# Transposes of normalised tokens in a two-layer encoder: handed back by the normalisation and placed among the dense products

## The chip, the cores and the metric

The kernel runs on one core of one Trainium2 chip. TensorE (PE in the profile) multiplies matrices and transposes; VectorE (DVE), ScalarE (ACT) and GpSimd (POOL) do elementwise work; SyncE (SP) issues most transfers. Each engine executes its own list of instructions in order and waits on semaphores for the others. The metric is the device time of one execution in microseconds (us).

## The reference

The reference normalises the input and runs two layers. A layer feeds the normalised tokens to three branches (pooling, differential attention with a relative-position bias, and a bidirectional RWKV-7 time mix), gates and merges them, projects, adds the residual and normalises; then a squared-ReLU MLP, residual and normalisation again:

```python
x = layer_norm(x, ln0_g, ln0_b)
for l in range(DEPTH):
    mix = hybrid_mixer(x, w_in[l], ...)
    x = layer_norm(alpha * x + mix, ln1_g[l], ln1_b[l])
    hid = jnp.square(jax.nn.relu(jnp.einsum('bsd,df->bsf', x, w_up[l])))
    x = layer_norm(alpha * x + jnp.einsum('bsf,fd->bsd', hid, w_down[l]), ln2_g[l], ln2_b[l])
```

There are 512 tokens, width 1024, an MLP of width 4096; all in float32.

## The kernel before

Every wide product is computed three times over with split operands: `split` (lines 142 and 143) makes a high part on ScalarE and the remainder on VectorE or GpSimd, and `mm3` (lines 181 to 183) issues high times high, high times low and low times high. The dense products need the tokens with the channels on the partitions: `self.xh` and `self.xl`, eight tiles of 128 channels by 512 tokens.

Three stages make these tokens anew: the end of `project` in layers 0 and 1, and the end of `mlp` in layer 0. All work alike. `token_tiles` runs the last products of four token tiles (128 tokens each; 24 products of 512 columns a tile) and calls `finish` after each, which calls `ln_tile`. That adds the residual with the row sums (line 238, VectorE), takes squares (L243, ScalarE), forms the scale (L245, L247, GpSimd), and writes the normalised row in two halves of 512 channels. For tiles 0 to 2 the first half is done by VectorE (L249, L256) and the second by GpSimd in three products (L252 to L254); tile 3 is done by VectorE alone. For each half four transposes follow on TensorE (L262, into one bank of PSUM), a cast to `xh` on ScalarE (L267) and a subtraction to `xl` on VectorE (L268). The banks of the four tiles are d l, a t, d l, a c, so that "d<-cst,s" in a row is the first half of tile 0 or 2.

Behind `token_tiles` stands `dense_halves`: three dense products (banks d, l, a), first for tokens 0 to 255, which need tiles 0 and 1, then for tokens 256 to 511. That is 2 x 3 x 24 = 144 products of 256 columns. In `mlp` these are the low-rank inputs of the next layer; `rw_prep` takes them over with `shift`, applies tanh and splits them with `lora_inputs` (L571 to L573), and goes on to the dense products for keys, inputs and values.

The order on each engine is not that of the code. The program is handed to a scheduler that simulates its own timeline and lays down every engine's list; the code's order is one of its inputs. Pools with a fixed number of buffers (`acc` takes the banks in turn) add waits for the last reader of a buffer.

Of the kernel before, what the change touches and what calls it, by code (L numbers as in the profile page):

```python
# [13 lines left out]
AF = mybir.ActivationFunctionType  # L14
ALU = mybir.AluOpType
# [7 lines left out]
NT = S // 128  # L23
DFF = 4096
# [6 lines left out]
LN_EPS = 1e-5  # L31
# [16 lines left out]
ALL_BANKS = "dlatdlac"  # L48
# [73 lines left out]
class Enc:  # L122
# [73 lines left out]

    def dense_halves(self, wts, tags="dl"):

        wts = [next(wts) for _ in tags]
        pss = [self.acc(t) for t in tags]  # L200
        for h in range(2):
            t = slice(h * 256, h * 256 + 256)
            for ps, (wh, wl) in zip(pss, wts):
                for k in range(NK):
                    if isinstance(wh, list):
                        h, l = wh[k // 4][:, k % 4, :], wl[k // 4][:, k % 4, :]
                    else:
                        h, l = wh[:, k, :], wl[:, k, :]
                    self.mm3(ps[:, t], h, l, self.xh[:, k, t], self.xl[:, k, t], k == 0, k == NK - 1)
        return pss  # L210
# [15 lines left out]

    def ln_tile(self, L, s, add, gb, it, eps, dst, transpose=True, banks="tc", bufs=2, pool=False):

# [21 lines left out]
        for h in range(2):  # L250
# [6 lines left out]
            if dst is not None:  # L257
                nc.sync.dma_start(dst[it * 128:(it + 1) * 128, half[h]], s[:, half[h]])
            if transpose:
                ps = self.acc(banks[h])  # L260
                for k in range(4):
                    nc.tensor.transpose(ps[:, k * 128:(k + 1) * 128], s[:, (h * 4 + k) * 128:(h * 4 + k + 1) * 128],  # L262
                                        self.ident)
                pv = ps.rearrange("p (k t) -> p k t", k=4)
                xh = self.xh[:, h * 4:h * 4 + 4, it * 128:(it + 1) * 128]
                xl = self.xl[:, h * 4:h * 4 + 4, it * 128:(it + 1) * 128]
                A.copy(xh, pv)  # L267
                V.tensor_tensor(xl, pv, xh, ALU.subtract)  # L268


    def run(self):
        tc, nc, a = self.tc, self.nc, self.a
        V, A, G = nc.vector, nc.scalar, nc.gpsimd
        with ExitStack() as ctx:
# [14 lines left out]
            with tc.tile_pool(name="LW", bufs=1, side="right") as LW, tc.tile_pool(name="L0", bufs=1, side="right") as L:  # L289
# [13 lines left out]
                for it in range(2):  # L303
                    self.ln_tile(L, ss[it], None, gb, it, LN_EPS, self.xs, banks=("tc", "ll")[it], bufs=NT, pool=it == 1)
                wts = [self.split(raws[i], [128, NK, 128], LW, "w", 3, G) for i in range(3)]
                for it in range(2, NT):
                    self.ln_tile(L, ss[it], None, gb, it, LN_EPS, self.xs, banks=("aa", "tc")[it - 2], bufs=NT)
                self.early = [self.wload(a["w_in"][0][:, COL_Z + i * 128:COL_Z + (i + 1) * 128], NK, 128) for i in (4, 0)]
# [156 lines left out]
    def rw_prep(self):  # L465
# [5 lines left out]
        pss = self.lora_ps  # L471
# [11 lines left out]
        yield 10.4  # L483
        tl = self.shift(pss[0], 12, self.F, "mg", 8)
        A.activation(tl, tl, AF.Tanh)
        tl = self.lora_inputs("tl", tl)
        la = self.lora_inputs("la", self.shift(pss[1], 13, self.F, "mg", 8))
        zg = self.shift(pss[2], 14, self.F, "mg", 8)
        A.activation(zg, zg, AF.Tanh, scale=0.5)
        V.tensor_scalar(self.sg, zg, 0.5, 0.5, ALU.mult, ALU.add)  # L490
        yield 5.2
        kw, rw, vw = (self.zcols(4 * i, 4) for i in (1, 0, 2))
        for j in range(4):
# [5 lines left out]
            yield 5.6  # L499
            if j == 0:  # L500
                ws = self.T(self.F, [128, 4, S], "ybh", 1, F32R)
                w2 = self.lora_weights([ws[:, i] for i in (0, 1)], a["rw_w2"][l])
                a2 = self.lora_weights([ws[:, i] for i in (2, 3)], a["rw_a2"][l])
# [719 lines left out]

    def token_tiles(self, X, xs, src, r0, finish, ahead):


        wr = []
        for k2 in range(0, 4, 2):
            for n in range(2):
                raw = self.wload(src[r0 + k2 * 128:r0 + (k2 + 2) * 128, n * 512:(n + 1) * 512], 2, 512)  # L1230
                wr.append(self.split(raw, [128, 2, 512], X, "wr", 4, self.nc.gpsimd))
        ahead()
        for it in range(NT):
            t = slice(it * 128, it * 128 + 128)
            for n in range(2):
                for k in range(4):
                    wh, wl = wr[k // 2 * 2 + n]
                    self.mm3(self.accs[it][n], xs[k][0][:, t], xs[k][1][:, t], wh[:, k % 2, :], wl[:, k % 2, :], False, k == 3)
            finish(it)

    def project(self):
# [21 lines left out]
        def finish(it):  # L1263
            self.ln_tile(L, self.s[it], self.accs[it], gb, it, 4.0 * LN_EPS, None, True,
                         ALL_BANKS[2 * it:2 * it + 2], pool=it < 3)

        with tc.tile_pool(name=f"W{l}", bufs=1) as X:
# [3 lines left out]

            self.token_tiles(X, self.mgr[4:], a["w_out"][l], 512, finish, ahead)
            self.up_ps = self.dense_halves(iter(self.ahead), "dla")

    def mlp(self):
# [4 lines left out]
        with tc.tile_pool(name=f"H{l}", bufs=1) as H, tc.tile_pool(name=f"M{l}", bufs=1) as M:  # L1280
            gb = self.ln_params(L, a["ln2_g"][l], a["ln2_b"][l])
            for half in range(2):
# [43 lines left out]
                def finish(it):  # L1326
                    self.ln_tile(L, self.s[it], self.accs[it], gb, it, LN_EPS, self.out[0] if last else self.xs, not last,
                                 ALL_BANKS[2 * it:2 * it + 2], pool=it < 3)

# [4 lines left out]

                self.token_tiles(M, hid[-4:], a["w_down"][l], DFF - 512, finish, ahead)
                if not last:
                    self.lora_ps = self.dense_halves(iter(self.ahead), "dla")

# [30 lines left out]
```

## Time and profile before

| | |
|---|---|
| median of three timed runs | 2115.34 us (2114.27 to 2118.49) |
| profiled execution | 2121.15 us |
| its span | 2119.4 us |
| TensorE busy | 2024.2 us, 96% of the span |
| TensorE's mean granted clock | 0.971 of full speed |

The span is the profiled time from first to last instruction. A row of a timeline gives the start, the duration and the instruction; in brackets stands how long the engine had been idle and who released it. Durations of matmuls overlap, so the distance between two starts is what one costs.

### The profile page before, as it was taken

How to read it: one execution, taken by the hardware profiler on the slowest of the kernel's cores; microseconds unless marked ns; L12 is line 12 of the kernel's file. 1: busy time of each engine (PE TensorE's matmuls, PEld its weight loads, DVE VectorE, ACT ScalarE, POOL GpSimd, SP SyncE). 2: the span in 40 equal slices, each digit the busy share in tenths (PEclk: the TensorE clock that was granted, in tenths of full speed). 3: DMA queues.
4: the chain of work that ended last, by engine and by line, in shares of the span. 5: the costliest groups of instructions: out<-in, count | busy, mean ns of one | idle time of the engine just before them, and what ended most of it. 6: DMA issues, size and time to landing. Idle time of an engine off the chain costs nothing.

```text
span 2119.4 us, 32782 instructions
## 1 busy us (share of the span) xinstructions
PE 2024.2 (96%) x13502; PEld 1647.4 (78%) x13502; DVE 1017.7 (48%) x1672; ACT 855.4 (40%) x1345; POOL 642.3 (30%) x447
## 2 busy tenths in 40 slices
PE   7999999899999999999989998989999999999998
PEld 5777778677787888888777676877777878888886
DVE  5775854445404542343348739454356045423433
ACT  5544554554233332232335336454532333312322
POOL 4555412122545200000536543021225561000004
PEclk9999989999999999999999999789999999999999
DMA  6446213455444233332424562135553442333322
GB/s 210 154 149 215 86 50 92 125 159 151 120 166 122 59 92 100 92 97 96 148 80 153 156 193 76 31 97 154 145 152 114 153 119 67 93 100 91 98 96 84
DMA packets 319042, 250.70 MB, mean 118 GB/s; under 512 B 51146, under 2 KB 278920, under 8 KB 318892
## 3 DMA queue, kind: packets, MB, share of 16 engines
q1 hardware_dynamic: 318748, 248.34, 38.8%
q8 instruction: 106, 1.74, 0.3%
q10 hardware_dynamic: 144, 0.26, 0.1%
q14 instruction: 44, 0.36, 0.1%
HBM read 208.70 MB, written 39.86 MB: 117 GB/s over the span
## 4 chain that ended last, share of the span: by engine, by line
PE 71%; DVE 11%; POOL 5%; ACT 4%; DMA 4%; issue 3%; SPq 1%; POOLq 0%; DVEq 0%; ACTq 0%
PE d L181 13%; PE d L183 13%; PE d L182 13%; PE l L181 3%; PE l L182 3%; PE l L183 3%; PE a L171 2%; PE c L171 2%; PE a L162 2%; PE a L181 1%; PE a L182 1%; PE a L183 1%; DVE x L674 1%; PE t L171 1%; DVE at L672 1%
## 5 line engine op out<-in xcount | busy, mean ns | idle before, releaser
L181 PE MATMUL d<-xh,wh 128*128 128x512 f32 (+1 forms) x1360 | 542.3, 399 | 13.1 <-DVE kl L975 4.9
L183 PE MATMUL d<-xh,wl 128*128 128x512 f32 (+1 forms) x1360 | 540.2, 397 | 4.1 <-POOL wl L143 4.1
L182 PE MATMUL d<-xl,wh 128*128 128x512 f32 (+1 forms) x1360 | 540.8, 398 | 0.0
L142 ACT CAST wh<-wraw 128x1024 fp32r<-128x1024 f32 x259 | 271.8, 1049 | 602.1 <-PE d L182 163.9
L143 POOL TENSOR_TENSOR wl<-wraw,wh 128x1024 fp32r<-128x1024 f32 x137 | 337.6, 2468 | 447.9 <-ACT wh L142 409.5
L143 DVE TENSOR_TENSOR wl<-wraw,wh 128x1024 fp32r<-128x1024 f32 x122 | 160.8, 1318 | 368.0 <-ACT wh L142 368.0
L181 PEld LDWEIGHTS d<-xh,wh 128*128 128x128 f32 x1360 | 260.6, 192 | 76.4 <-issue 9.7
L183 PEld LDWEIGHTS d<-xh,wl 128*128 128x128 f32 x1360 | 260.6, 192 | 65.6 <-POOL wl L143 5.1
L182 PEld LDWEIGHTS d<-xl,wh 128*128 128x128 f32 x1360 | 260.8, 192 | 58.7 <-issue 0.5
L143 POOL TENSOR_TENSOR wrl<-wraw,wrh 128x1024 fp32r<-128x1024 f32 x16 | 40.2, 2528 | 659.6 <-ACT wrh L142 659.6
L1294 ACT CAST hh<-f 128x512 fp32r<-128x512 f32 x64 | 39.7, 621 | 84.5 <-DVE f L1291 84.5
L1001 ACT ACTIVATE p<-p,mx 128x512 f32<-128x512 f32 x64 | 46.1, 721 | 51.7 <-DVE mx L1000 51.6
L1295 DVE TENSOR_TENSOR hl<-f,hh 128x512 fp32r<-128x512 f32 x64 | 44.2, 693 | 41.4 <-ACT hh L1294 41.3
L999 DVE CUSTOM_DVE_ANT_0 p<-l,tb 128x512 f32<-128x512 f32 x64 | 43.2, 685 | 30.8 <-PE l L996 29.0
L1218 DVE SCALAR_TENSOR_TENSOR ybh<-ybh,d 128x512 f32<-128x512 f32 x4 | 2.8, 688 | 101.8 <-PE d L183 101.7
L1291 DVE TENSOR_TENSOR f<-f 128x512 f32<-128x512 f32 x64 | 43.6, 685 | 14.9 <-ACT f L1290 14.9
L672 DVE TENSOR_TENSOR at<-x 128x60 f32<-128x60 f32 (+14 forms) x60 | 48.3, 804 | 1.7
L183 PE MATMUL l<-wh,hl 128*128 128x512 f32 x112 | 43.6, 389 | 0.0
L182 PE MATMUL d<-wl,hh 128*128 128x512 f32 x112 | 43.6, 389 | 0.0
L183 PE MATMUL d<-wh,hl 128*128 128x512 f32 x112 | 43.6, 389 | 0.0
L182 PE MATMUL l<-wl,hh 128*128 128x512 f32 x112 | 43.6, 389 | 0.0
L182 PE MATMUL a<-wl,hh 128*128 128x512 f32 x112 | 43.6, 389 | 0.0
(521 smaller groups left out, 3938.6 us busy)
## 6 DMA issues: line engine op xcount, KB each, us to landing
wraw<-in_w_in_dram SPq DMA_DIRECT2D x110, 512.0 KB
wraw<-in_w_up_dram SPq DMA_DIRECT2D x64, 512.0 KB
wraw<-in_w_down_dram SPq DMA_DIRECT2D x64, 512.0 KB
sc<-st SPq DMA_DIRECT2D x16, 1280.0 KB
ch<-sc SPq DMA_DIRECT2D x32, 640.0 KB
wraw<-in_w_branch_dram SPq DMA_DIRECT2D x24, 512.0 KB
gd<-f SPq DMA_DIRECT2D x32, 256.0 KB
wraw<-in_w_out_dram SPq DMA_DIRECT2D x16, 512.0 KB
```

What stands on the lines that cost most here:

```text
L142: self.nc.scalar.copy(hi, src)
L143: (eng or self.nc.vector).tensor_tensor(lo, src, hi, ALU.subtract)
L162: self.anchor = self.nc.tensor.matmul(*args, **kw).ins
L171: i = self.nc.tensor.matmul(*args, **kw).ins
L181: mm(out, wh, xh, start=first, stop=False)
L182: mm(out, wh, xl, start=False, stop=False)
L183: mm(out, wl, xh, start=False, stop=last)
L672: V.tensor_tensor(w, ab[:, s + 1:, :, s].unsqueeze(3).to_broadcast([128, n, 2, s]), ab[:, s, :, :s].unsqueeze(1).to_broadcast([128, n, 2, ...
L999: V.tensor_tensor_reduce(p, ps, bias, op0=ALU.add, op1=ALU.max, scale=1.0, scalar=-3e38, accum_out=mx)
L1001: A.activation(p, p, AF.Exp, bias=mx, accum_out=sm[:, m:m + 1])
L1291: V.tensor_tensor(f, f, f, ALU.mult)
L1295: V.tensor_tensor(lo, f, hi, ALU.subtract)
```

## The change

`ln_tile` no longer issues the transposes. It returns a function `turn` that issues both halves, transposes, casts and subtractions together. The first normalisation calls it at once. `token_tiles` collects the functions and calls tile 0's ahead of tile 3's products; `dense_halves` calls tile 1's ahead of its first product, tile 2's ahead of the third product of the first half, and tile 3's ahead of the second half. In `rw_prep` the tanh and splits of the low-rank inputs stand behind the first key tile.

```diff
-    def dense_halves(self, wts, tags="dl"):
+    def dense_halves(self, wts, tags="dl", turns=None):
         wts = [next(wts) for _ in tags]
+        if turns:
+            turns[1]()
         pss = [self.acc(t) for t in tags]
...
+                if turns and half == 0 and i == 2:
+                    turns[2]()
+                if turns and half == 1 and i == 0:
+                    turns[3]()
...
-            if transpose:
+
+        def turn():
+            for h in range(2):
                 ps = self.acc(banks[h])
...
                 A.copy(xh, pv)
                 V.tensor_tensor(xl, pv, xh, ALU.subtract)
+
+        return turn
...
-        tl = self.shift(pss[0], 12, self.F, "mg", 8)
-        A.activation(tl, tl, AF.Tanh)
-        tl = self.lora_inputs("tl", tl)
-        la = self.lora_inputs("la", self.shift(pss[1], 13, self.F, "mg", 8))
-        zg = self.shift(pss[2], 14, self.F, "mg", 8)
-        A.activation(zg, zg, AF.Tanh, scale=0.5)
-        V.tensor_scalar(self.sg, zg, 0.5, 0.5, ALU.mult, ALU.add)
+        tl, la, zg = (self.shift(pss[i], 12 + i, self.F, "mg", 8) for i in range(3))
...
             if j == 0:
+                A.activation(tl, tl, AF.Tanh)
+                tl = self.lora_inputs("tl", tl)
+                la = self.lora_inputs("la", la)
+                A.activation(zg, zg, AF.Tanh, scale=0.5)
+                V.tensor_scalar(self.sg, zg, 0.5, 0.5, ALU.mult, ALU.add)
...
+        turns = []
         for it in range(NT):
+            if it == 3 and turn:
+                turns[0]()
...
-            finish(it)
+            turns.append(finish(it))
+        return turns
```

On TensorE, in `project` of layer 0, before the change: the end of tile 3's products (c), tile 2's first transposes (d_6691), the first dense product's 24 rows (d_6762), and tile 2's second transposes (l_6701).

```order
L183 MATMUL c_6377<-wrh_6521,mrl_6351 128x512
L262 MATMUL d_6691<-cst_79,s_6364 128x128 x4
L181 MATMUL d_6762<-xh_63,wh_6527 128x256
L182 MATMUL d_6762<-xl_64,wh_6527 128x256
L183 MATMUL d_6762<-xh_63,wl_6528 128x256
...
L262 MATMUL l_6701<-cst_79,s_6364 128x128 x4
L181 MATMUL l_6763<-xh_63,wh_6533 128x256
```

The same place after the change:

```order
L183 MATMUL c_6377<-wrh_6521,mrl_6351 128x512
L271 MATMUL a_6720<-cst_79,s_6361 128x128 x4
L271 MATMUL t_6727<-cst_79,s_6361 128x128 x4
L181 MATMUL d_6734<-xh_63,wh_6527 128x256
L181 MATMUL l_6735<-xh_63,wh_6533 128x256
L271 MATMUL d_6785<-cst_79,s_6364 128x128 x4
L271 MATMUL l_6792<-cst_79,s_6364 128x128 x4
L181 MATMUL a_6736<-xh_63,wh_6539 128x256
L182 MATMUL d_6734<-xl_64,wh_6527 128x256
```

Tile 2's second transposes (l) stood behind 24 dense products and now stand behind two; tile 1's (a, t) stood among tile 3's products and now stand behind them. Tile 0's, not shown, moved behind seven more products of 512 columns. Layer 1 has the same rows.

On TensorE at the end of `mlp` in layer 0, before, where tile 1's second transposes are t_9068 and tile 2's d_9114 and l_9125, with twelve dense products between the last two:

```order
L183 MATMUL c_8546<-wrh_8927,hl_8536 128x512
L262 MATMUL t_9068<-cst_79,s_6361 128x128 x4
L262 MATMUL d_9114<-cst_79,s_6364 128x128 x4
L181 MATMUL d_9188<-xh_63,hh_8933 128x256
L182 MATMUL d_9188<-xl_64,hh_8933 128x256
...
L262 MATMUL l_9125<-cst_79,s_6364 128x128 x4
L181 MATMUL l_9189<-xh_63,hh_8943 128x256
```

and after:

```order
L183 MATMUL c_8546<-wrh_8927,hl_8536 128x512
L271 MATMUL a_9146<-cst_79,s_6361 128x128 x4
L271 MATMUL t_9153<-cst_79,s_6361 128x128 x4
L181 MATMUL d_9160<-xh_63,hh_8933 128x256
L181 MATMUL l_9161<-xh_63,hh_8943 128x256
L271 MATMUL d_9211<-cst_79,s_6364 128x128 x4
L181 MATMUL a_9162<-xh_63,hh_8953 128x256
L271 MATMUL l_9218<-cst_79,s_6364 128x128 x4
L182 MATMUL d_9160<-xl_64,hh_8933 128x256
```

Three dense products instead of twelve run ahead of tile 2's second transposes. In all three stages tile 3's two groups, which stood within the third dense product, now stand side by side ahead of the second half. On GpSimd, in this stage only, two memsets (`rs`, L476 before) moved ahead of tile 2's last product.

On VectorE at the start of layer 1's `rw_prep`, after the change: the shift of the third low-rank input (mg), the low-rank remainders (kl), the gate (sg) and the first key tile (k).

```order
L461 SCALAR_TENSOR_TENSOR mg_9370<-a_9162,par_79_483,mg_9370 128x511
L583 TENSOR_TENSOR kl_9439<-mg_9362,tl_9437 64x512
L583 TENSOR_TENSOR kl_9440<-mg_9362,tl_9438 64x512
L583 TENSOR_TENSOR kl_9451<-mg_9366,la_9449 64x512
L583 TENSOR_TENSOR kl_9452<-mg_9366,la_9450 64x512
L510 TENSOR_SCALAR sg_9353<-mg_9370 128x512
L460 SCALAR_TENSOR_TENSOR k_9405<-d_9380,par_79_483,k_9405 128x511
L461 SCALAR_TENSOR_TENSOR k_9405<-d_9380,par_79_483,k_9405 128x511
```

Before the change the same operations stood in the same order (L450, four of L573, L490, L449, L450): nothing moved here, nor on ScalarE, nor in layer 0. What else moved is layer 1 from the triangular solve of `rw_solve` on: there TensorE, VectorE, ScalarE and SyncE have the same operations in another order up to the merge of the branches, and the dense products stand at other places between the small products of the solve.

## Rows read from the trace of the kernel before

**Rows 1.** The page: busy time, share of the span and instructions of each engine.
```profile
PE 2024.2 (96%) x13502; PEld 1647.4 (78%) x13502; DVE 1017.7 (48%) x1672; ACT 855.4 (40%) x1345; POOL 642.3 (30%) x447
```

**Rows 2.** Waits of TensorE: waiter, releaser, us in total, times, longest.
```profile
PE d L262 <- DVE s L256: 6.2, 5, 2.3
...
PE d L181 <- DVE k L450: 3.2, 1, 3.2
```

**Rows 3.** Timeline of TensorE, `project` of layer 0: start, duration, instruction.
```profile
689.46 0.66 PE L262 MATMUL d<-cst,s 128*128 128x128 f32 x4 [1.52 <-DVE s L256]
...
692.82 0.66 PE L262 MATMUL l<-cst,s 128*128 128x128 f32 x4 [1.31 <-POOL s L254]
...
701.62 0.28 PE L182 MATMUL d<-xl,wh 128*128 128x256 f32 x1
...
704.35 0.60 PE L262 MATMUL l<-cst,s 128*128 128x128 f32 x4
```

**Rows 4.** Timeline of GpSimd in the same stage.
```profile
691.51 1.26 POOL L254 TENSOR_TENSOR s<-s,lngb 128x512 f32<-128x512 f32 x1
...
694.12 1.32 POOL L252 TENSOR_SCALAR s<-s,lnnm,lnr 128x512 f32<-128x512 f32 x1
...
699.64 0.78 POOL L252 TENSOR_SCALAR s<-s,lnnm,lnr 128x512 f32<-128x512 f32 x1
...
702.17 1.30 POOL L254 TENSOR_TENSOR s<-s,lngb 128x512 f32<-128x512 f32 x1
```

**Rows 5.** Timelines of GpSimd and TensorE, `project` of layer 1.
```profile
1756.43 1.31 POOL L254 TENSOR_TENSOR s<-s,lngb 128x512 f32<-128x512 f32 x1
...
1758.60 0.60 PE L262 MATMUL l<-cst,s 128*128 128x128 f32 x4
```

**Rows 6.** Timelines of TensorE and GpSimd, end of `mlp` in layer 0.
```profile
1061.94 0.66 PE L262 MATMUL d<-cst,s 128*128 128x128 f32 x4 [1.36 <-DVE s L256]
...
1065.32 0.66 PE L262 MATMUL l<-cst,s 128*128 128x128 f32 x4 [0.65 <-POOL s L254]
...
1063.98 1.29 POOL L254 TENSOR_TENSOR s<-s,lngb 128x512 f32<-128x512 f32 x1
1065.21 0.35 POOL L476 MEMSET rs<- 128x128 f32 x2
```

**Rows 7.** The same stage, tile 3: transposes, cast and subtraction on their engines.
```profile
1070.06 0.60 PE L262 MATMUL a<-cst,s 128*128 128x128 f32 x4
...
1070.70 0.59 ACT L267 CAST xh<-a 128x512 fp32r<-128x512 f32 x1 [4.10 <-PE a L262]
...
1071.32 0.69 DVE L268 TENSOR_TENSOR xl<-a,xh 128x512 fp32r<-128x512 f32 x1 [2.66 <-ACT xh L267]
```

**Rows 8.** Timeline of TensorE in layer 1, then two stretches (granted clock behind PEld, DVE, ACT, POOL).
```profile
1743.71 0.66 PE L262 MATMUL d<-cst,s 128*128 128x128 f32 x4 [2.34 <-DVE s L256]
...
1744.00:1748.00 4.00, 3.71 (x15) 2.66 (x14) 2.65 (x5) 1.71 (x3) 3.75 (x5) 0.57 0.00 0
690.00:694.00 4.00, 2.69 (x15) 1.97 (x14) 2.57 (x6) 2.20 (x4) 3.75 (x5) 1.00 0.00 0
```

**Rows 9.** The chain that ended last: start, duration, piece; layer 0 and layer 1.
```profile
303.56 3.07 PE a L162 x58
...
640.70 2.33 DVE wl L143
...
1351.08 3.07 PE a L162 x58
...
1693.83 2.33 DVE wl L143
```

**Rows 10.** Timeline of TensorE in layer 1's solve, wide products: first two, last of 29.
```profile
1356.77 0.63 PE L181 MATMUL d<-xh,wh 128*128 128x512 f32 x1
1357.20 0.63 PE L182 MATMUL d<-xl,wh 128*128 128x512 f32 x1
...
1378.71 0.62 PE L183 MATMUL l<-ybh,yal 128*128 128x512 f32 x1
```

More of the change, by code (lines that the diff above doesn't have):

```diff
@@ L195, in quarters @@
         return his, los
-    def dense_halves(self, wts, tags="dl"):
+    def dense_halves(self, wts, tags="dl", turns=None):
         wts = [next(wts) for _ in tags]
+        if turns:
+            turns[1]()
         pss = [self.acc(t) for t in tags]
-        for h in range(2):
-            t = slice(h * 256, h * 256 + 256)
-            for ps, (wh, wl) in zip(pss, wts):
+        for half in range(2):
+            t = slice(half * 256, half * 256 + 256)
+            for i, (ps, (wh, wl)) in enumerate(zip(pss, wts)):
+                if turns and half == 0 and i == 2:
+                    turns[2]()
+                if turns and half == 1 and i == 0:
+                    turns[3]()
                 for k in range(NK):
@@ L225, in ln_params, with ln_tile @@
         return gb
-    def ln_tile(self, L, s, add, gb, it, eps, dst, transpose=True, banks="tc", bufs=2, pool=False):
+    def ln_tile(self, L, s, add, gb, it, eps, dst, banks="tc", bufs=2, pool=False):
         nc = self.nc
@@ L303, in run @@
                 for it in range(2):
-                    self.ln_tile(L, ss[it], None, gb, it, LN_EPS, self.xs, banks=("tc", "ll")[it], bufs=NT, pool=it == 1)
+                    self.ln_tile(L, ss[it], None, gb, it, LN_EPS, self.xs, banks=("tc", "ll")[it], bufs=NT, pool=it == 1)()
                 wts = [self.split(raws[i], [128, NK, 128], LW, "w", 3, G) for i in range(3)]
                 for it in range(2, NT):
-                    self.ln_tile(L, ss[it], None, gb, it, LN_EPS, self.xs, banks=("aa", "tc")[it - 2], bufs=NT)
+                    self.ln_tile(L, ss[it], None, gb, it, LN_EPS, self.xs, banks=("aa", "tc")[it - 2], bufs=NT)()
                 self.early = [self.wload(a["w_in"][0][:, COL_Z + i * 128:COL_Z + (i + 1) * 128], NK, 128) for i in (4, 0)]
@@ L1221, in merged, with token_tiles @@
         self.mgr.append(self.split(self.mg[m], [128, S], self.MR, "mr", NK, (V, G)[m % 2]))
-    def token_tiles(self, X, xs, src, r0, finish, ahead):
+    def token_tiles(self, X, xs, src, r0, finish, ahead, turn=True):
         wr = []
@@ L1263, in finish @@
         def finish(it):
-            self.ln_tile(L, self.s[it], self.accs[it], gb, it, 4.0 * LN_EPS, None, True,
-                         ALL_BANKS[2 * it:2 * it + 2], pool=it < 3)
+            return self.ln_tile(L, self.s[it], self.accs[it], gb, it, 4.0 * LN_EPS, None,
+                                ALL_BANKS[2 * it:2 * it + 2], pool=it < 3)
         with tc.tile_pool(name=f"W{l}", bufs=1) as X:
@@ L1270, in ahead @@
                                          "w", 2, nc.gpsimd) for i, pool in enumerate((self.MR, self.MR, self.P))]
-            self.token_tiles(X, self.mgr[4:], a["w_out"][l], 512, finish, ahead)
-            self.up_ps = self.dense_halves(iter(self.ahead), "dla")
+            turns = self.token_tiles(X, self.mgr[4:], a["w_out"][l], 512, finish, ahead)
+            self.up_ps = self.dense_halves(iter(self.ahead), "dla", turns)
     def mlp(self):
@@ L1326, in finish @@
                 def finish(it):
-                    self.ln_tile(L, self.s[it], self.accs[it], gb, it, LN_EPS, self.out[0] if last else self.xs, not last,
-                                 ALL_BANKS[2 * it:2 * it + 2], pool=it < 3)
+                    return self.ln_tile(L, self.s[it], self.accs[it], gb, it, LN_EPS, self.out[0] if last else self.xs,
+                                        ALL_BANKS[2 * it:2 * it + 2], pool=it < 3)
                 def ahead():
@@ L1333, in ahead @@
                         self.ahead = [self.quarters(H, src[:, i * 128:(i + 1) * 128]) for i in range(3)]
-                self.token_tiles(M, hid[-4:], a["w_down"][l], DFF - 512, finish, ahead)
+                turns = self.token_tiles(M, hid[-4:], a["w_down"][l], DFF - 512, finish, ahead, not last)
                 if not last:
-                    self.lora_ps = self.dense_halves(iter(self.ahead), "dla")
+                    self.lora_ps = self.dense_halves(iter(self.ahead), "dla", turns)
 _INS = ['x', 'ln0_g', 'ln0_b', 'w_in', 'pool_w', 'pool_scale', 'da_lambda', 'da_subln_g', 'rel_bias',
```

## The prediction

> **What bounds the kernel now.** I read the busy shares first. TensorE works 96% of the span [rows 1], so a change pays only where it takes a wait from TensorE or lets it run at its upper clock. Its waits, read next, show which ones the edit can reach [rows 2]: transposes that wait for the normalised tokens (6.2 us in the group of those that wait for VectorE), and one wait of 3.2 us for a shifted key tile of layer 1. The transposes stand in three stages: the ends of `project` in layer 0 (about 687 to 712 us) and layer 1 (1741 to 1766), and the end of `mlp` in layer 0 (1052 to 1074). In these I read the timelines of TensorE and GpSimd side by side. TensorE executes its rows in order, so a transpose that waits holds back everything behind it.
>
> What is to be seen in layer 0's `project`: TensorE stops twice for tile 0, 1.52 us before the first transposes and 1.31 us before the second [rows 3]. The second halves come from GpSimd, which works through the tiles with hardly a gap: tile 0's last product begins at 691.51 and ends at 692.77, tile 2's begins at 702.17 and ends at 703.47 [rows 4]. So tile 2's second half cannot be transposed before about 703.5, wherever its transposes stand in TensorE's queue. Before the change TensorE reaches them at 704.35, with no wait, because 24 dense products of 256 columns were run between tile 2's two groups of transposes [rows 3].
>
> **The change, part by part.** No operation is added or removed; each stage still has eight groups of four transposes, with one cast on ScalarE and one subtraction on VectorE each, and no DMA in the moved step. What counts is the order.
>
> *Tile 0 in `project`.* Seven products of 512 columns now run ahead of tile 0's first transposes instead of behind them. They fill the first wait of 1.52 us. But tile 0's second half is ready at 692.77 as before, so the wait reappears there: TensorE is done with the seven products and the first transposes at about 690.1 and waits some 2.7 us. TensorE passes this point at the same moment, having done one product more (0.2 us). That lead is worth nothing, because the next item holds it up again.
>
> *Tile 2 in `project`.* In the new order both groups of tile 2 stand behind the first two dense products. Tile 3's 24 products and tile 1's transposes end near 700; one cast later the two dense products run, tile 2's first transposes follow, and the second ones wait for GpSimd until 703.52. That is 0.83 earlier than 704.35, but 142 of the 144 dense products are still to do, where 120 were left before. One of them takes 0.119 (2.73 us for the 23 steps from 701.62 to 704.35 [rows 3]), so the 22 cost 2.61. Net +1.78. In layer 1 GpSimd is done at 1757.74 and TensorE was there at 1758.60 [rows 5]: 2.61 − 0.81 = +1.80.
>
> *Tile 2 in `mlp`.* Here the second transposes already waited for GpSimd and began at 1065.32 [rows 6], with 132 dense products left. Now 141 are left: 9 × 0.119 = 1.07. GpSimd also gets two memsets (0.35 together) ahead of the last product of tile 2, which moves 1065.27 to 1065.62. Net +1.42.
>
> *Tile 3, all three stages.* Its two groups now stand together, directly ahead of the second half of the dense products. From the start of a group to the end of the cast it takes 1.23 us, to the end of the subtraction 1.95 [rows 7]. The second group covers 0.72 of the 1.28 until the first product may start, leaving 0.56; the four products that need only the cast then reach just to the subtraction. Before, dense products stood between the groups and nothing waited. 3 × 0.56 = +1.7. Sum of the stages: 1.78 + 1.80 + 1.42 + 1.68 = **+6.7**.
>
> *The clock.* [...] In four busy microseconds 0.57 loses 4 × 0.43 = 1.7 us. In `mlp` the new wait before tile 2's second transposes runs from about 1062.6 to 1065.7, 3 us, with dense work right behind: I charge **+1.7**. In the two `project` stages the long wait is tile 0's, and what a low clock loses there is hidden by the later wait for GpSimd, which then shrinks to about 1 us; I charge nothing and keep 0 to 1.7 each for the range. [...]
>
> *The low-rank inputs.* Their tanh, casts and subtractions stand later in the code, but the rows of VectorE and ScalarE around them are in the same order in both layers; the third fence of the section on the change shows it. The wait of 3.2 us stays: 0. If it did go, −3.2.
>
> *Layer 1's solve.* From the triangular solve on, the scheduler orders layer 1 differently, though nothing in that code changed. The same code takes different times in the two layers: from the same point of the solve to the last splits ahead of `project` it is 337.14 us in layer 0 and 342.75 in layer 1, 5.6 more [rows 9]. In layer 1 dense products of 512 columns run inside the solve, where the clock is low: one per 0.43, against twice 0.119 at the upper clock; there are 29 from the first to the last of [rows 10]. The new order has four between the small products and then some twelve until the clock can rise, close to layer 0's order: 13 fewer × 0.19 = **−2.5**. Bounds: −5.6, all that separates the layers, and +4, about what a wait like 3.2 us would add with the clock it costs. I take −2.5, the part that rows price.
>
> **The sum.** 6.7 + 1.7 − 2.5 = +5.9 us. The profiled execution took 2121.15 (span 2119.4 and 1.75 around it), so it would take 2127.1. It lies 5.8 above the median of the three timed runs, 2115.34; on these I expect 2121.2. About 0.2% (4.2 us) is what a measurement of this kernel can tell from no change.
>
> **Rivals.**
> 1. *The new order of layer 1 pays back the stages.* If its solve and attention become as quick as layer 0's (−5.6) and the clock in `mlp` holds, 6.7 − 5.6 = +1.1: 2116.4. For it: the start of the new order matches layer 0's row by row. Against: the later part matches neither layer.
> 2. *GpSimd's floor drops, and the transposes stop waiting: faster.* Place: tile 2's second half. One GpSimd product of tile 2 took 0.78 where its like for tile 1 took 1.32 [rows 4]. If all eight heavy products behind the first ran like that (8 × 0.54 = 4.3 us), the floor would lie ahead of TensorE, which then reaches tile 2's second transposes near 700.9: 3.4 earlier than now, less 2.61 and 0.56, −0.2 in each `project`, and in `mlp` 2.8 earlier, less 1.07 and 0.56, −1.2. The point from which it decides is a floor 2.6 us lower. With layer 1 like layer 0 it comes to −7.2: 2108.1. Against: of tile 0's and tile 2's last products the rows show 1.26 and 1.30, whatever stands beside them. [...]
> 3. *The clock falls in every stage.* 2 × 1.7 more: +9.3, 2124.6. For it, the 2.34 us wait of layer 1; against, the smaller second waits.
>
> **How the numbers follow.** Forecast with rival 3 (net over +4.2): 0.57. Near zero, mostly rival 1: 0.31. Faster, rival 2 or a luckier layer 1: 0.12. Low end of the range: 2113, between rivals 1 and 2, to take in a lower floor or a layer 1 that gains more than layer 0's order; high end: 2127, rival 3 with layer 1 gaining nothing (6.7 + 1.7 + 3.4 = 11.8). The likeliest case alone spans 2119.5 to 2127.
>
> **What will show it.** In the profile of the changed kernel: in each `project` one wait of about 2.7 us for GpSimd at tile 0's second transposes, and one of 1 to 2.7 at tile 2's; the last dense product of the stage about 2.3 us later against the start of GpSimd's chain. In `mlp` a wait of about 3 us at tile 2's second transposes and a granted clock well under 1 behind it. At tile 3 about 0.56 idle before the second half. The 3.2 us wait for the key tile unchanged. Between the solve's last small products and the last splits of layer 1, about 340 us instead of 342.75. The prediction is wrong if GpSimd ends tile 2 much before 703.5 counted from the same start, if the scheduler's rows are not what TensorE meets in order, or if layer 1's new order moves the time by more than the stages do.

## The result and the profile after

The changed kernel took 2135.8 us (median of five, 2130.49 to 2141.77), the kernel before 2118.49 beside it (median of five): a ratio of 1.0085, interval 1.0072 to 1.0099. It is slower, as forecast, but by some 18 us (the ratio times 2118) where +5.9 was the sum, and it lies above the range. The profiled execution took 2141.77 us, its span is 2140.0, 20.6 more than the span before.

Page of the changed kernel: busy time by engine, and the granted clock in 40 slices.

```profile
PE 2041.9 (95%) x13502; PEld 1659.5 (78%) x13502; DVE 1013.1 (47%) x1672; ACT 853.5 (40%) x1345; POOL 640.0 (30%) x447
...
PEclk9999978999999999999999999699999999999999
```

The same 13502 matmuls keep TensorE busy for 17.7 us more than in [rows 1], while the other engines are busy slightly less. Of the 20.6 us TensorE's idle time has only 2.9 (98.1 against 95.2 us). For the most part TensorE did not wait, it ran slower: the mean clock is 0.963, before 0.971.

The chain that ended last, at the places of [rows 9] (start, duration, piece).

```profile
308.56 3.07 PE a L162 x58
...
645.79 2.32 DVE wl L143
...
1360.18 3.07 PE a L162 x58
...
1711.82 2.33 DVE wl L143
```

With [rows 9] these rows cut the 20.6 us into stretches. Up to layer 0's solve: +5.0 (308.56 − 303.56). From there to its last splits: +0.1. From these over layer 0's `project` and `mlp` to layer 1's solve: +4.0 (714.39 against 710.38). Layer 1 from the solve to its last splits: 351.64 against 342.75, **+8.9**. From there to the end, with layer 1's `project`: +2.6. The last three are the change's; the first is not (low_rank_alone below).

Timeline of TensorE in layer 0's `project` after the change, to be read beside [rows 3].

```profile
694.66 0.66 PE L271 MATMUL d<-cst,s 128*128 128x128 f32 x4
...
697.98 0.92 PE L271 MATMUL l<-cst,s 128*128 128x128 f32 x4 [2.67 <-POOL s L261]
...
708.77 0.66 PE L271 MATMUL l<-cst,s 128*128 128x128 f32 x4 [0.90 <-POOL s L261]
...
718.71 0.39 PE L181 MATMUL d<-xh,wh 128*128 128x256 f32 x1 [0.24 <-ACT xh L276]
```

The waits of 1.52 and 1.31 became one of 2.67 at tile 0's second transposes and 0.90 at tile 2's. The last row is the first product of the second half of the dense products. Before the change it is this one:

```profile
711.28 0.28 PE L181 MATMUL d<-xh,wh 128*128 128x256 f32 x1
```

Counted from the last splits of the solve (645.79 and 640.70) it starts 2.34 later than before, which is just the 1.78 + 0.56 of the prediction. At tile 3 TensorE idles only 0.24, counted from the modelled end of the second group. By starts, tile 3's two groups take 1.28 up to that product (717.43 to 718.71), where each took 0.36 before, among the dense products: 0.56 more, as forecast.

Timeline of TensorE at the end of `mlp`, beside [rows 6]:

```profile
1072.92 1.11 PE L271 MATMUL l<-cst,s 128*128 128x128 f32 x4 [2.67 <-POOL s L261]
...
1074.47 0.41 PE L182 MATMUL d<-xl,hh 128*128 128x256 f32 x1
1074.68 0.41 PE L183 MATMUL d<-xh,hh 128*128 128x256 f32 x1
```

Stretches of 4 us after the long wait, in `project` and in `mlp` (granted clock behind POOL's share):

```profile
698.00:702.00 4.00, 4.00 (x13) 3.29 (x14) 3.85 (x9) 1.68 (x3) 3.69 (x4) 0.57 0.00 0
1073.00:1077.00 4.00, 4.00 (x19) 4.00 (x20) 3.59 (x6) 0.59 (x1) 1.36 (x2) 0.50 0.35 131
```

Behind both waits the clock, 0.57 and 0.50 of full speed, is at or near its lower level: the products start 0.21 apart in `mlp`, where 0.119 is the distance at the upper one. From 1350 to 1400 us, by half microseconds, the granted clock is 1.00 or 0.50 before and after the change, with other values only where it passes from one to the other; these are the two levels meant below.

Layer 1 from a copy of its solve (VectorE, x<-c) to the last splits, and 40 us from its start. The rows of this form in the next section, where they begin behind 1340 us, are the same stretch of their kernel: start and end, length, then busy time and count of PE, PEld, DVE, ACT, POOL, then the granted clock. In the 40 us TensorE is busy throughout, and all of it at a clock of 0.50.

```profile
1354.64:1711.82 357.18, 342.20 (x3304) 279.28 (x3305) 140.01 (x320) 145.18 (x255) 106.78 (x73) 0.91 0.42 122
...
1354.00:1394.00 40.00, 40.00 (x494) 34.42 (x494) 11.83 (x24) 10.64 (x21) 0.00 (x0) 0.50 0.06 17
```

The same place in the old order, from a run below (low_rank_alone), where a part of it is at the upper level:

```profile
1343.50:1383.50 40.00, 40.00 (x495) 34.36 (x495) 11.06 (x23) 12.76 (x25) 0.00 (x0) 0.58 0.06 16
```

### The profile page after: what moved, and what is told of

The parts are those of the page before. It is cut to its first block, busy times and chain, and to the rows that moved or that the text cites. A ratio compares the mean times of both kernels' runs of the same rounds, so it can differ in the third digit from the quotient of the medians.

```text
span 2140.0 us, 32782 instructions
## 1 busy us (share of the span) xinstructions
PE 2041.9 (95%) x13502; PEld 1659.5 (78%) x13502; DVE 1013.1 (47%) x1672; ACT 853.5 (40%) x1345; POOL 640.0 (30%) x447
## 4 chain that ended last, share of the span: by engine, by line
PE 72%; DVE 11%; POOL 5%; ACT 4%; DMA 4%; issue 4%; SPq 0%; POOLq 0%; DVEq 0%; ACTq 0%
PE d L181 13%; PE d L183 13%; PE d L182 13%; PE l L181 3%; PE l L182 3%; PE l L183 3%; PE a L171 2%; PE a L162 2%; PE c L171 2%; PE a L181 1%; PE a L182 1%; PE a L183 1%; DVE x L684 1%; ACT wh L142 1%; PE t L171 1%
## 5 line engine op out<-in xcount | busy, mean ns | idle before, releaser
L171 PE MATMUL a<-ch 64*128 64x128 f32 x512 | 43.6, 295 | 0.1
```

Of the source, the lines that this page charges most:

```text
L171: i = self.nc.tensor.matmul(*args, **kw).ins
```

## The experiments

Three theories stood against each other when the result was known. A: the order that the scheduler gave layer 1 is slow by itself. B: layer 1 is slow because it starts later or colder behind the moved transposes. C: one unlucky profile. D and E came later: that any other order than the old one is slower, and that the moves themselves help.

The handle on them: moving single tiles in layer 0 makes the scheduler lay out layer 1 in yet other orders, and some sets of tiles give the old or the changed order. In the kernels below a tile is moved if it is in a set, and else transposed half by half as before ("p" is `project`, "m" is `mlp`, then layer and tile):

```diff
+LATE = {("p", 0, 0), ...}
...
+            if not late:
+                flip(h)
...
         def turn():
-            for h in range(2):
-                ps = self.acc(banks[h])
+            if late:
+                for h in range(2):
+                    flip(h)
```

`flip` holds what `turn` held for a half; `finish` passes `late=("p", l, it) in LATE`.

**low_rank_alone.** The kernel before with only the last part of the change's diff:

```diff
-        tl = self.shift(pss[0], 12, self.F, "mg", 8)
-        A.activation(tl, tl, AF.Tanh)
-        tl = self.lora_inputs("tl", tl)
...
+        tl, la, zg = (self.shift(pss[i], 12 + i, self.F, "mg", 8) for i in range(3))
...
             if j == 0:
+                A.activation(tl, tl, AF.Tanh)
+                tl = self.lora_inputs("tl", tl)
```

> The kernel before with the move of the low-rank inputs alone. Every engine has the same list of instructions as before, so all theories expect no change within 0.2% (4.2 us), and the 3.2 us wait for the key tile of layer 1 again. What it tells apart is the first 300 us: the changed kernel's profile shows them 5.0 us longer than the profile of before, although the lists there are the same. If that is a matter of the single execution (which short stretches run at the lower clock), this profile puts the layer-0 solve's chain piece somewhere between 303.5 and 309 us with other stretches at the lower clock; if it came from the change, it stands at 303.5.

Measured: 2118.14 us against 2118.08, ratio 1.0003 (0.9984 to 1.0022). The low-rank move changes no list of an engine, and no cost is seen. And with the same list of instructions on every engine its twelve runs lie between 2111.3 and 2127.4 us. Its profile reaches the layer-0 solve 1.0 us later than that of before; the changed kernel, profiled a second time, reaches it as early as before. These are the two profiles of the changed kernel, from the start to a copy in layer 0's solve, first the one above, then after_again:

```profile
0.00:310.11 310.11, 282.87 (x1685) 224.87 (x1686) 204.39 (x331) 163.01 (x273) 147.74 (x106) 0.95 0.48 147
```

```profile
0.00:305.03 305.03, 280.83 (x1685) 223.83 (x1686) 205.37 (x331) 163.57 (x273) 148.01 (x106) 0.97 0.49 150
```

The same 1685 matmuls, 5.1 us and 0.02 of the clock apart: the front's +5.0 belongs to the execution, not to the change. The following row is layer 1's stretch here, in the old order:

```profile
1344.18:1688.70 344.52, 330.43 (x3304) 271.58 (x3305) 145.35 (x319) 145.77 (x255) 107.94 (x73) 0.94 0.44 127
```

**one_stage_alone.** Against the kernel before:

```diff
+LATE = {("p", 1, 0), ("p", 1, 1), ("p", 1, 2), ("p", 1, 3)}
```

> Transposes moved in layer 1's project alone; all other lists are as before. By the prediction's terms the stage costs 1.80 for tile 2 and 0.56 for tile 3: +2.4 us, +0.11%. The profile of the changed kernel shows this stage 2.0 us longer (the offset to before goes from 18.0 to 20.0). A rival in which the front's 5 us belong to the program and not to the execution has nothing to add here. In the profile: waits of 2.7 us for GpSimd at tile 0's second transposes, and layer 1's solve to last splits in 342.7 us.

Measured: 2120.69, ratio 1.0016 (1.0000 to 1.0032), +3.4 us by the ratio, as in all that follows, and hardly to be told from none. All lists up to this stage are those of before. From a split ahead of the stage to VectorE's last instruction the profile has 380.1 us against 377.5: +2.6, near the forecast of 2.4.

**all_but_one_tile.** Against the changed kernel, with `LATE` of all twelve tiles:

```diff
-LATE = {("p", 0, 0), ("p", 0, 1), ("p", 0, 2), ("p", 0, 3), ...}
+LATE = {("p", 0, 0), ("p", 0, 1), ("p", 0, 2), ...}
```

> The changed kernel, but tile 3 of layer 0's project is transposed as before, half by half. The scheduler then gives layer 1's solve, attention and merge the order of before, while all other moves stay. Theory A (the new order of layer 1 costs 8.9 us by itself): solve to last splits in about 343 us, and a time of 2135.8 - 8.9 - 0.6 = 2126 us, +0.37% on before. Theory B (the 8.9 us follow from the later or colder start of layer 1 after the moved transposes, not from its order): solve to last splits near 351 us and 2135 us.

Measured: 2135.51, ratio 1.0079 (1.0051 to 1.0107), 9 us over theory A. But the layer-1 stretch took 345.25 us, as with the old order, although it began 7.6 us later than in the changed kernel's profile: there theory B falls. Five of the missing 9 us are a wait that the edit itself made. Timeline of TensorE in layer 0's `project`:

```profile
706.98 0.60 PE L246 MATMUL t<-cst,s 128*128 128x128 f32 x4
712.50 1.97 PE L246 MATMUL a<-cst,s 128*128 128x128 f32 x8 [4.92 <-DVE s L278]
```

Tile 3 is now written ahead of tile 1's late transposes and takes its bank first, so tile 1's first half and all dense products wait 4.92 us for tile 3's normalisation. The stage costs 7.6 us more than unmoved (391.73 against 384.17 from layer 0's last splits to a split in `mlp`), where the four moved tiles cost 2.6. What the other 4 are is not shown; the interval of the measured +16.7 us, 10.8 to 22.7, is wide enough for them.

**new_order_few_moves.** Against the kernel before:

```diff
+LATE = {("p", 0, 1), ("p", 0, 2)}
```

> Only tiles 1 and 2 of layer 0's project are moved; the scheduler answers with the changed kernel's order of layer 1's solve, attention and merge, row for row on TensorE. Theory A: solve to last splits in about 351.6 us, so +8.9 and at most 1.8 for tile 2: about +10 us, +0.47%, 2128.5. Theory B: only the stage's price, +1.8 at most, 2120, and solve to last splits near 343.

Measured: 2137.55, ratio 1.0096 (1.0074 to 1.0119). Layer 1's stretch took 353.88 us at a clock of 0.92: theory A again, with two moved tiles instead of twelve. 7.4 of the rest are the same wait for a bank as above (391.61 in that stretch).

**after_again.** The changed kernel without an edit.

> The changed kernel once more, for a second profile of it and a comparison on the same chip as the others of this call. Theory A (the new order of layer 1 is slow by itself, because 140 small products of the solve stand in a row with no wide product among them, so the clock stays low): solve to last splits again 9 to 12 us longer than in kernels with the old order, TensorE at the lower clock for 57 to 64 us of it (41 to 51 us in four profiles of the old order). Time +0.8% on before, 2135. Theory C (the order is harmless and the one profile of the changed kernel was unlucky): solve to last splits within 3 us of the 348 of before's profile.

Measured: 2136.03, ratio 1.0085 (1.0068 to 1.0102); layer 1's stretch 354.33 us, clock 0.92. Theory C falls.

**mlp_two_tiles_as_before.** Against the changed kernel:

```diff
-LATE = {..., ("m", 0, 0), ("m", 0, 1), ("m", 0, 2), ("m", 0, 3)}
+LATE = {..., ("m", 0, 2), ("m", 0, 3)}
```

> The changed kernel, but tiles 0 and 1 at the end of layer 0's mlp are transposed as before; by the prediction's terms these two are worth nothing. The scheduler answers with another order of layer 1: 7 wide products, 68 small ones, 19 wide, 64 small, 12 wide, where the changed kernel has 6 wide, 140 small, 20 wide. Theory A: the clock comes back in between, 41 to 51 us low, solve to last splits as with the old order, and about 10 us less than the changed kernel: +0.35%, 2126. Theory D (any order but the old one is slower, for its waits and not for the clock): about as slow as the changed kernel, 2135.

Measured: 2117.18, ratio 0.9997 (0.9984 to 1.0010): ten of the twelve moves are in place and the whole loss is gone, even more than theory A had it. Its stretch:

```profile
1346.37:1685.48 339.11, 326.57 (x3304) 268.61 (x3304) 145.04 (x319) 145.52 (x255) 107.43 (x73) 0.95 0.44 129
```

**without_mlp_moves.** Against the changed kernel:

```diff
-LATE = {..., ("m", 0, 0), ("m", 0, 1), ("m", 0, 2), ("m", 0, 3)}
+LATE = {...}
```

> The changed kernel with all four tiles of mlp as before; the moves in both project stages stay. The scheduler gives a third order of layer 1: 8 wide, 68 small, 18 wide, 64 small, 12 wide. By the terms that held, two stages at 2.0 to 2.5 us: +4.7. Theory A: nothing more, +0.22%, 2123. Theory D: about 10 us more, 2133.

Measured: 2114.14, ratio 0.9981 (0.9970 to 0.9992): faster than before by 4.0 us where theory A had +4.7. Its stretch took 334.56 us at 0.95, shorter than any with the old order. Theory D falls, and A's figure for this order was too high.

This kernel and the one before it have the changed kernel's rows in layer 0's `project`, but in their profiles the clock stayed at its upper level there (the transposes behind the first wait take 0.66 in the row below, 0.92 in the changed kernel's). The two waits for GpSimd in mlp_two_tiles_as_before:

```profile
692.66 0.66 PE L246 MATMUL l<-cst,s 128*128 128x128 f32 x4 [2.68 <-POOL s L276]
...
703.47 0.66 PE L246 MATMUL l<-cst,s 128*128 128x128 f32 x4 [2.48 <-POOL s L276]
```

The first wait is as long as in the changed kernel, the second 2.48 where that had 0.90, and the stage takes as long, from layer 0's last splits to a split in `mlp`: 386.9 and 386.6 us here, 386.7 to 387.1 in the three profiles with the low clock. So what the low clock loses in `project` is hidden by the second wait, as the prediction had it.

**one_tile_in_mlp.** Against the kernel before:

```diff
+LATE = {("m", 0, 3)}
```

> Tile 3 of mlp alone is moved (its two groups side by side), nothing else. By the prediction's terms +0.56 for the stage. Layer 1 gets a fourth order: 68 small, 8 wide, 64 small, 17 wide. Theory A: no run of more than 68 small products, so solve to last splits as with the old order and a time within 0.2% of before. Theory D: +10 us, 2128.

Measured: 2122.85, ratio 1.0031 (1.0018 to 1.0044), +6.6 us: neither theory's number. The stretch:

```profile
1345.05:1695.92 350.87, 333.61 (x3304) 272.97 (x3305) 144.06 (x320) 145.38 (x255) 107.27 (x73) 0.93 0.43 125
```

It is 5.7 us longer than the mean of the old order, 2.6 longer than the longest of its six profiles. Of the 5.7, 3.5 are waits: 350.87 − 333.61 = 17.3 us idle, where the six profiles of the old order have 13.8 in the mean. An order can cost by waits too; theory A as I had put it, by the clock and runs of small products alone, was too narrow.

**first_stage_alone** and **two_single_tiles.** Against the kernel before, the one and the other:

```diff
+LATE = {("p", 0, 0), ("p", 0, 1), ("p", 0, 2), ("p", 0, 3)}
```

```diff
+LATE = {("p", 0, 3), ("m", 0, 3)}
```

> The kernel before with the four tiles of layer 0's project moved and nothing else. Layer 1 gets the order of the kernel without the mlp moves (8 wide, 68 small, 18 wide, 64 small, 12 wide). Theory A (what an order costs is half its time at the lower clock plus TensorE's waits): layer 1's solve to last splits near 335 us, about 10 less than the mean of four profiles of the old order, and the stage +2.4: 8 us less than before, -0.38%, 2109. Rival E (the kernel without the mlp moves was 0.19% faster because the transposes that were moved in project help, and its layer 1 was lucky): it then lies at -0.1% or nearer to before, 2115 or more, with solve to last splits near 345.

> Only tile 3 of layer 0's project and tile 3 of its mlp are moved: +1.1 by the prediction's terms. The start of layer 1's solve has the same runs as in the run just above (68 small, 18 wide, 64 small, 12 wide), the later part other rows. Theory A: solve to last splits 335 to 340, 5 to 9 us less than before, 2108 to 2112: a version that beats both kernels. Rival: the later part brings waits (16.4 us of TensorE's waits in the run with one tile in mlp, against 8.0 without the mlp moves) and the time is that of before, 2117.

Measured: 2109.51, ratio 0.9966 (0.9950 to 0.9981), and 2111.56, ratio 0.9972 (0.9958 to 0.9986). Both beat both kernels, by what theory A gave. The two stretches, of the first and of the second:

```profile
1346.32:1678.59 332.27, 322.76 (x3304) 264.65 (x3304) 140.55 (x319) 146.02 (x255) 108.30 (x73) 0.96 0.46 132
```

```profile
1349.05:1685.09 336.04, 325.22 (x3304) 266.43 (x3304) 141.46 (x320) 145.68 (x255) 108.19 (x73) 0.95 0.44 130
```

Rival E falls: two single tiles, whose moves gain little or nothing in their stages (383.99 against 384.17 us in the stretch with `project`; 56.1 from a split in `mlp` to its last dense product, where kernels with nothing moved there take 56.6 to 58.0), give nearly the same gain through layer 1's order.

**stage_tile3** and **stage_tiles23.** Against the kernel before:

```diff
+LATE = {("p", 1, 3)}
```

```diff
+LATE = {("p", 1, 2), ("p", 1, 3)}
```

> In layer 1's project tile 3 alone is transposed in the new place; layer 1's order before that is the old one. Read from the trace alone, as the stage's length between the last splits ahead of it and the next split behind it. By the prediction +0.56; a rival in which tile 3 costs nothing, since its transposes are ready early, gives 0.

> The same with tiles 2 and 3. By the prediction 0.56 + 1.80 = +2.36, so nearly all of the 2.5 that the stage costs with four tiles; by a rival in which tile 0's long wait and the clock behind it are the price, 0.6 to 1.

One run each, read from the profiles alone. From a split ahead of the stage to the last dense product, before, tile 3, tiles 2 and 3, and all four (one_stage_alone): 36.08, 37.81, 35.93 and 38.69 us. The time at the lower clock in it was 3.4, 6.8, none and 3.4 us; take half of that off, roughly what it lost, and it is 34.4, 34.4, 35.9 and 37.0. So tile 3 costs nothing in sum, tiles 2 and 3 about 1.5, and the step to four tiles 1.1 more; with one profile each, these are estimates. In sum only: at its own place tile 3 has its price in stage_tile3 too (1.27 from its first transposes, at 1763.61, to the first product of the second half, where the two groups took 0.71 before). But the scheduler now runs dense products of the third bank ahead of tile 2's first transposes, and their wait of 0.47 is gone. Timelines of TensorE, tile 2's two groups, with tiles 2 and 3 moved and with all four:

```profile
1759.72 0.60 PE L246 MATMUL d<-cst,s 128*128 128x128 f32 x4
1760.15 0.60 PE L246 MATMUL l<-cst,s 128*128 128x128 f32 x4
```

```profile
1752.52 0.60 PE L246 MATMUL d<-cst,s 128*128 128x128 f32 x4
1754.05 0.65 PE L246 MATMUL l<-cst,s 128*128 128x128 f32 x4 [0.93 <-POOL s L276]
```

Counted from the same split they start at 22.39 and at 18.25. Where tiles 0 and 1 stay, the scheduler puts tile 2 behind more dense products, and it waits for nobody. The wait at tile 2 arises only where tiles 0 and 1 are moved as well. In `mlp` it is much the same: with tiles 2 and 3 moved and 0 and 1 not (mlp_two_tiles_as_before), tile 2's second transposes do not wait, and the time from a split in `mlp` to the last of its dense products is 56.0 us, not longer than the 56.6 to 58.0 of kernels in which nothing moved there.

## Why the prediction failed: layer 1's order, taken with the wrong sign

The direction was right, but the stages on which the forecast rested make some 8 us of the loss; the larger part comes from layer 1, which had been entered as a gain. The last three stretches of the section on the result hold, by profiles, what the edits cost. For layer 1 there are enough profiles to set orders beside each other (length, TensorE busy and clock as in the rows above; "wide" are products of 512 columns; a small product of the order is about two instructions in the profile, which counts the 140 as 276):

| order of layer 1, start of the solve | profiles | length, us | TensorE busy | clock |
|---|---|---|---|---|
| old: 8 wide, 64 small, 11 wide, 68 small, 19 wide | 6 | 342.5 to 348.3, mean 345.2 | mean 331.4 | 0.93 to 0.94 |
| changed: 6 wide, 140 small, 20 wide | 3 | 353.9 to 357.2, mean 355.1 | mean 340.5 | 0.91 to 0.92 |
| mlp_two_tiles_as_before | 1 | 339.1 | 326.6 | 0.95 |
| without_mlp_moves, first_stage_alone | 2 | 334.6, 332.3 | 325.4, 322.8 | 0.95, 0.96 |
| two_single_tiles | 1 | 336.0 | 325.2 | 0.95 |
| one_tile_in_mlp | 1 | 350.9 | 333.6 | 0.93 |

The first row is before, low_rank_alone, one_stage_alone, all_but_one_tile, stage_tile3 and stage_tiles23; the second after, after_again and new_order_few_moves. In every profile TensorE does 3304 matmuls in the stretch. The changed order costs 9.9 us, of which 9.1 are busy time: TensorE does the same work more slowly. Waits are 0.8 of it.

Two things make it slower, and the timelines show both. TensorE in the changed order, within the solve:

```profile
1368.68 0.63 PE L181 MATMUL d<-xh,wh 128*128 128x512 f32 x1
1369.24 3.27 PE L162 MATMUL a<-x,at 32*32 32x32 f32 x61
...
1380.44 0.79 PE L171 MATMUL a<-ch 64*128 64x128 f32 x2
1381.17 0.31 PE L162 MATMUL t<-tt,x 32*32 32x32 f32 x2
1381.40 0.79 PE L171 MATMUL a<-ch 64*128 64x128 f32 x2
...
1394.10 0.60 PE L181 MATMUL l<-ybh,yal 128*128 128x512 f32 x1
1394.53 0.42 PE L182 MATMUL l<-ybl,yal 128*128 128x512 f32 x1
```

and in first_stage_alone:

```profile
1359.81 2.40 PE L165 MATMUL a<-x,at 32*32 32x32 f32 x61
...
1366.89 0.62 PE L185 MATMUL d<-xl,wh 128*128 128x512 f32 x1
1367.32 0.42 PE L186 MATMUL d<-xh,wl 128*128 128x512 f32 x1
...
1378.83 1.16 PE L174 MATMUL a<-ch 64*128 64x128 f32 x16
1379.92 1.19 PE L165 MATMUL t<-tt,x 32*32 32x32 f32 x32
```

*The clock.* In the changed order a row of 61 small instructions takes 3.27 us, in the other 2.40, and the wide ones pass from 0.43 apart to 0.23 apart at 1394.5 in the one and at 1367.3 in the other, during a row of wide products both times. In these timelines of the solve it rose only in or right behind rows of wide products, and in first_stage_alone it was lost in a row of small ones with TensorE busy throughout. These stand there before and behind 3.9 us of small products:

```profile
1369.91 0.39 PE L185 MATMUL d<-xl,wh 128*128 128x512 f32 x1
1370.14 0.40 PE L186 MATMUL d<-xh,wl 128*128 128x512 f32 x1
...
1374.99 0.63 PE L185 MATMUL l<-ybl,yal 128*128 128x512 f32 x1
1375.41 0.63 PE L186 MATMUL l<-ybh,yal 128*128 128x512 f32 x1
```

The wide products are 0.23 apart ahead of them and 0.42 behind. The row of 40 us at 0.50 in the section on the result says the same: busy throughout and never at the upper level; the other two profiles of this order have the same row at 0.50, and low_rank_alone, in the old order, has 0.58 in its place. With two levels, 1.00 and 0.50, a mean clock c over L us is 2 x (1 − c) x L at the lower one, and I take half of it as lost, an estimate: a wide product costs 0.43 against 0.23, 16 of a<-ch 2.10 (low_rank_alone, 1387.53 to 1389.63) against 1.09 (first_stage_alone, 1378.83 to 1379.92), 32 small ones 1.82 (low_rank_alone, 1363.06 to 1364.88) against 1.03 (first_stage_alone, 1379.92 to 1380.95). That loses 29.6 us in the mean of the changed order, 22.8 of the old (by unrounded clocks), so about 7 of the 9.1. The same order does not always fare the same: the old one has 41 to 51 us at the lower level in its six profiles, the changed one 57 to 64.

*Alternating shapes.* The changed order deals out 14 of the products a<-ch (64x128) in pairs between pairs of small ones: 0.96 per round, 6.5 us from 1380.44 to the last. In first_stage_alone 16 of them stand together and take 1.09. At the lower clock, 16 took 2.10 and 32 small ones 1.82 (low_rank_alone, as above), so gathered the 14 and 12 would take 2.5: the alternation costs about 4.0. As those 6.5 us lie in the low stretch too, the two overlap: 4.0 for the alternation would leave 5.1 of the 9.1 for the rest of the low clock. This split is an estimate from rows; no run took one of the two away alone. Why a pair costs more between others is not shown.

Now the prediction's steps in turn.

- *Sum of the stages, +6.7, and +1.7 for the clock in `mlp`.* The size held, mostly: +2.6 in each `project` (forecast 1.78 or 1.80, and 0.56; in layer 0 also by the means, 386.8 against 384.2 us), and in `mlp` +3.0 where 3.7 was the sum, 1.42, 0.56 and 1.7 for the clock (the loss in 4 us at the 0.57 of [rows 8]; the 4 us behind the wait in `mlp` had 0.50): from a split in it to the last of its 144 dense products 60.5, 60.0 and 59.9 us in after, after_again and all_but_one_tile, 57.2 in the mean of the eight profiles with an unmoved `mlp`, 56.6 to 58.0. Up to layer 1's solve it is +2.1 (322.3 against 320.2 in the mean), but behind the stage the lists are the same. The 2.67 us waits came as foreseen. In `project` the clock fell behind them in some profiles and not in others (0.92 and 0.66 for the transposes behind the wait, as above), hidden either way by the wait for GpSimd.
- *Its split by tiles* held for the change as a whole, 2.34 at the second half of layer 0's `project`, but the terms are not the tiles' own: moved without tiles 0 and 1, tile 2 waits for nobody, and where tile 3 alone is moved, its 0.56 is paid back at tile 2.
- *Low-rank inputs, 0; the 3.2 us wait stays.* Right: in the waits of TensorE after the change (the second row) it stands as it did in [rows 2].

```profile
PE l L271 <- POOL s L261: 9.9, 5, 2.7
...
PE d L181 <- DVE k L461: 3.2, 1, 3.2
```

- *Layer 1's solve, −2.5, bounds −5.6 and +4.* This step failed: +9.9. I charged the wide products in the solve for what each loses at the lower clock, 0.19, and counted 13 fewer as a gain. But among the small products it is in rows of wide ones that the clock came back, in the timelines above. The small products, whose time the low clock stretches too (32 of them from 1.03 to 1.82), were not in the sum. The upper bound was one wait of another kind with its clock; nothing in it stood for a solve that stays low throughout. That the start matched layer 0's order was taken as a sign of layer 0's time, but the match ends where it matters. In layer 0, before the change, the last of the first wide products and the next row of them, fourteen:

```profile
314.91 0.63 PE L181 MATMUL d<-xh,wh 128*128 128x512 f32 x1
...
322.63 0.78 PE L182 MATMUL d<-xl,wh 128*128 128x512 f32 x1
```

There 7.2 us of small products (68) stand between the two, and the clock rises within the fourteen (0.43 apart up to 324.06, 0.23 from 324.48 on); in layer 1's changed order it is 140, from 1369.24 to 1390.10, 20.9 us.

- *Rival 1, layer 1 pays back the stages*, was wrong for the order that the change got and right for its neighbours: 9 to 13 us less than the old order in three kernels, 6 in a fourth.
- *Rival 2*, a lower GpSimd floor, did not occur: tile 2's last product on GpSimd in layer 0's `project` ends at 708.71, where 703.47 and the 5.09 between the last splits give 708.56. *Rival 3*, the clock in every stage, is half seen: in both profiles of the changed kernel it fell in every stage (in the first to 0.57 and 0.50 in the stretches above, and to 0.52 from 1763 to 1767 us in layer 1's `project`), and `mlp` alone shows a cost that it can explain; the same wait in `project`, 2.68 us, left the clock at its upper level in two other kernels.

The terms as measured add up to the times within 5 us, which is what a single profile of layer 1 allows (the old order's own spread is 5.8 us). For the old and the changed order the mean of the table above stands, for the others their own profile:

| kernel | stages | layer 1, length − 345.2 | sum, us | measured, ratio − 1 times 2118 |
|---|---|---|---|---|
| changed | 2.6 + 2.6 + 3.0 | +9.9 | +18.1 | +18.0 |
| new_order_few_moves | 7.4 | +9.9 | +17.3 | +20.3 |
| all_but_one_tile | 7.6 + 2.6 + 3.0 | 0 | +13.2 | +16.7 |
| one_stage_alone | 2.6 | 0 | +2.6 | +3.4 |
| mlp_two_tiles_as_before | 2.6 + 2.6 | −6.1 | −0.9 | −0.6 |
| one_tile_in_mlp | 0 | +5.7 | +5.7 | +6.6 |
| without_mlp_moves | 2.6 + 2.6 | −10.6 | −5.4 | −4.0 |
| two_single_tiles | 0 | −9.2 | −9.2 | −5.9 |
| first_stage_alone | 2.6 | −12.9 | −10.3 | −7.2 |

Left open: how much of the +9.9 a solve in the changed order would lose with the alternation taken out alone, and why orders with the same start differ in their later waits.

## What to carry to other kernels

Where a scheduler lays out the lists, a small edit is also a throw of the dice for everything behind it: here the edit's own places cost some 8 us, and the order of code that nobody touched was worth from −13 to +10. Compare such an edit with neighbours that give other orders before judging it, and keep the best order apart from the edit. And do not price a wide product by its own time where the clock is low: ask what brings the clock back for the small ones behind it (here 32 of them took 1.82 at the lower level and 1.03 at the upper).

## What the runs showed that was not expected

- TensorE was busy without a gap, as far as the profile's busy time tells, and stayed at the lower level: 40.00 of 40.00 us busy at a clock of 0.50 in all three profiles of the changed order, the work being mostly products of 32x32.
- Kernels whose lists are the same to the last instruction spread over 20 us: before from 2108.25 to 2128.28 in 23 runs, low_rank_alone from 2111.3 to 2127.4 in twelve. The profiles differ in which short stretches ran at the lower clock; each of 3.4 us is worth some 1.5 us (the two fronts above: 11.4 us more at the lower clock, 5.1 us longer).
